# Low half of each split weight tile: negated high half from ScalarE plus an accumulating DMA, in place of a VectorE subtraction

## The chip, the core and the metric

The kernel runs on one core of one Trainium2 chip: TensorE (PE, matmuls, with its weight loads as PEld), VectorE (DVE), ScalarE (ACT), GpSimd (POOL) and SyncE (SP, which issues most DMAs), each with its own queue of instructions in a fixed order. The metric is the device time of one execution in microseconds; lower is better.

## The reference, cut to what matters

One decoder layer over 1024 tokens of width 1024 (`D_MODEL = SEQ = 1024`), in float32:

```python
h = rms_norm(x, g_norm)
proj = h @ w_in                       # RWKV, conv, attention inputs and merge gates: 97 tiles of 128 columns
y_rwkv = (o_rwkv * silu(rwkv_gate)) @ w_proj_rwkv      # after a scan over 16 heads of 64
y_conv = u @ w_proj_conv + b_proj_conv                 # after a causal depthwise conv of width 31
km, vm = split(rms_norm(mem, g_mem_norm) @ w_mem_kv)   # 256 memory tokens
y_mem = (att * silu(mem_gate)) @ w_proj_mem
y = gates[0] * y_rwkv + gates[1] * y_conv + gates[2] * y_mem
return x + y @ w_out                  # then a final rms_norm
```

## The kernel before, in words

All large matmuls are done to nearly float32 accuracy with operands rounded to fp32r: each operand is a sum of a high and a low half, and a product is three matmuls, high by high, high by low, low by high. For a weight tile `wf` (128 x 1024, 512 KB) the halves are `wh`, `wf` rounded to fp32r by an ACT copy, and `wl = wf - wh`.

A `Stream` (lines 131 to 163) brings weight tiles in a fixed order: `load` issues the DMA of `wf` on SP's queue, `split` makes `wh` and `wl`, `get` hands them to the matmuls, `ahead` prepares the next tile. There is one buffer for `wf` and two each for `wh` and `wl`, so the halves of tile n+1 go where those of tile n-1 were, and can be written only when the last matmul of tile n-1 is done. The main stream has 121 tiles; a second one (`kv_stream`, two `wf` buffers) has the 16 tiles of `w_mem_kv`.

`g_dense` (line 279) is one weight tile against 1024 tokens: two halves e of 24 matmuls of 512 columns (tile `d` in PSUM), called from generators that interleave it with other work. `g_kv` (line 867) uses a kv tile for only 24 matmuls of 256 columns (`g<-mH,wh`) or 12 of 512 (`ry<-wl,mH`). Instructions are handed over in the order in which the code runs, and a scheduler then sets the order on each engine.

The stages, by the profile's time: to about 49 us the norm of `x`; to about 1030 us the RWKV part, with its scan (`sav` L703, `sas` L710, `s` L713, group norm `vr` L114 and L118, `Y` L754, transposes L759) among dense tiles; then attention and the convolution, whose taps (`ac` L841) run on DVE and whose sum `csum` (L846, L848) on POOL, with the 16 kv tiles at 1059 to 1127 us; from about 1519 us the layer norm and the three branch projections with their loads; from about 1865 us the output projection.

Of the kernel before, what the change touches and what calls it, by code (L numbers as in the profile page):

```python
# [10 lines left out]
F32 = mybir.dt.float32  # L11
F32R = mybir.dt.float32r
AF = mybir.ActivationFunctionType
ALU = mybir.AluOpType
# [48 lines left out]
def hybrid_kernel(ctx: ExitStack, tc: tile.TileContext, x: bass.AP, mem: bass.AP, wt: bass.AP,  # L63
                  vecs: bass.AP, wup: bass.AP, gfin: bass.AP, out: bass.AP):
    nc = tc.nc
    act, dve, pool, pe = nc.scalar, nc.vector, nc.gpsimd, nc.tensor
# [7 lines left out]
    def bank(tag, bufs=1):  # L74
        return ps.tile([P, HS], F32, name=tag, tag=tag, bufs=bufs)
# [45 lines left out]
    def split_sb(src, hi, lo, scale=None, eng=None):  # L121
        if scale is None:
            act.copy(hi, src)  # L123
            (eng or dve).tensor_tensor(out=lo, in0=src, in1=hi.bitcast(F32), op=ALU.subtract)  # L124
        else:
            act.activation(hi, src, AF.Copy, scale=scale)
            dve.scalar_tensor_tensor(out=lo, in0=src, scalar=scale, in1=hi.bitcast(F32),
                                     op0=ALU.mult, op1=ALU.subtract)


    class Stream:
        def __init__(self, order, pl, raw=1, parts=2):
            self.order, self.n_dma, self.n_split, self.n_use = order, 0, 0, 0
            self.pl, self.bufs = pl, (raw, parts)
            self.raw, self.parts, self.eng = {}, {}, dve

        def load(self, upto):
            while self.n_dma < min(upto, len(self.order)):
# [5 lines left out]
        def split(self, upto):  # L144
            while self.n_split < min(upto, len(self.order)):
                self.load(self.n_split + 1)
                wh = self.pl.tile([P, D], F32R, name="wh", tag="wh", bufs=self.bufs[1])
                wl = self.pl.tile([P, D], F32R, name="wl", tag="wl", bufs=self.bufs[1])
                split_sb(self.raw.pop(self.n_split), wh, wl, eng=self.eng if self.n_split else dve)
                self.parts[self.n_split] = (wh, wl)  # L150
                self.n_split += 1

# [52 lines left out]
    stream = Stream(order, wp)  # L205
# [73 lines left out]
    def g_dense(idx, done, rh=None, rl=None, pre=None):  # L279
        wh, wl = stream.get(idx)  # L280
        rh, rl = (hH, hL) if rh is None else (rh, rl)
        for e in range(2):
            if pre is not None:
                pre(e)
            po = bank("d", 2)
            sl = slice(e * HS, (e + 1) * HS)
            n = 0
            for k in range(KT):
                ks_ = slice(k * P, (k + 1) * P)
                for l, r in ((wh, rh), (wh, rl), (wl, rh)):  # L290
                    pe.matmul(po, lhsT=l[:, ks_], rhs=r[:, k, sl], start=(n == 0), stop=(n == 3 * KT - 1))  # L291
                    n += 1
                    if n % 4 == 0 and n < 3 * KT:
                        yield
            if e == 0:
                stream.ahead()
            done(e, po)
            yield

# [20 lines left out]

    late = {}
    lo_gen = g_dense(T_LO, lambda e, po: late["lo"](e, po))
    with tc.tile_pool(name="prep", bufs=1, reuse_waits="tile") as pl:
        for i, _ in enumerate(g_norm(x, S, "g_norm", pl, hH, hL)):
# [4 lines left out]
    with tc.tile_pool(name="rk", bufs=1, reuse_waits="tile") as rk:  # L329
# [103 lines left out]
        def tile_job(kind, j):  # L433
            if kind == "lo":
                late["lo"] = done_lo
                return lo_gen
            if kind == "k":
                return g_dense(T_K + j, done_shift(KS, j, T_K, "ks", 2))
            if kind == "r":
                return g_dense(T_R + j, done_shift(RS, j, T_R, "rs", 3))  # L440
            if kind == "v":
                return g_dense(T_V + j, done_shift(VS, j, T_V, "v", 2))
            if kind == "g":
                return g_dense(T_RG + j, done_sg(j))
            return g_dense(T_M0 + j, done_m(j))
# [722 lines left out]
    with tc.tile_pool(name="wo1", bufs=1, reuse_waits="tile") as w1:  # L1168
# [12 lines left out]
        for fh in range(2):  # L1181
            fs = slice(fh * HS, (fh + 1) * HS)
            oh, ol = wo[fh]
            for t in range(KT):
# [10 lines left out]
                if fh == 1:  # L1195
                    rsqrt(rs[:, t:t + 1], ss[:, t, 1:2], 1.0 / D, e0[:, t:t + 1])
                    for h_ in range(2):
                        hs_ = slice(h_ * HS, (h_ + 1) * HS)
                        dve.scalar_tensor_tensor(out=xr[t][:, hs_], in0=xr[t][:, hs_], scalar=rs[:, t:t + 1],
                                                 in1=gf[:, hs_], op0=ALU.mult, op1=ALU.mult)  # L1200
# [46 lines left out]
```

## Time and profile before

| what | value |
|---|---|
| median of 3 runs (all) | 1961.22 us (1957.13, 1961.22, 1961.71) |
| the profiled execution, time and span | 1960.84 us, span 1959.0 us |
| mean granted TensorE clock | 0.991 |
| busy share of the span: PE, DVE, ACT, POOL | 94%, 72%, 35%, 12% |
| bytes read from HBM | 139.92 MB |
| `wh` copies on ACT, `wl` subtractions on DVE | 137 each |

A row of the profile names the line of the kernel, the engine, the operation, and what is written from what. A "busy" PE is one with a matmul in flight. Where a row of the timeline ends in [t <-X], the engine was idle for t us before it and X ended the wait.

### The profile page before, as it was taken

Reading aid. Unit: us, or ns where it says so; the run is one execution under the profiler, and the core shown is the slowest. Engines: PE = TensorE matmul, PEld = TensorE weight load, DVE = VectorE, ACT = ScalarE, POOL = GpSimd, SP = SyncE. Lnnn points to the kernel's source line nnn. Section 1 sums busy time; section 2 is a strip of 40 time slices with the busy share of each in tenths; the row PEclk is TensorE's granted clock in tenths of the full one; section 3 lists DMA queues with packets and bytes.
Section 4 is the critical chain, followed back from the end, with each engine's and each line's share of the span. In section 5 each row is a group of like instructions: output and inputs, shape, how many; then the busy total and the mean of one; then the engine's idle time right before and its main releaser. Section 6 shows DMA issues by size and latency. Waiting matters only on the chain. (4 is left out here: it accounts for less than half of the span.)

```text
span 1959.0 us, 30018 instructions
## 1 busy us (share of the span) xinstructions
PE 1848.2 (94%) x11412; PEld 1472.8 (75%) x11412; DVE 1411.1 (72%) x3028; ACT 693.2 (35%) x1303; POOL 226.5 (12%) x311
## 2 busy tenths in 40 slices
PE   6999998989899899989999999999999999999998
PEld 5777766767676676667788888888888787778887
DVE  6667787777778777787636998898999748644423
ACT  6334343443344344334334313232313435432121
POOL 2201111111111111111000000000000213100001
PEclk9999999999999999999999999999999999999999
DMA  4232212122121212212224411212123646775332
GB/s 147 58 97 63 71 36 68 54 61 68 48 86 36 66 56 58 71 42 79 71 78 140 132 46 42 75 54 76 54 76 108 233 163 221 256 252 164 129 129 86
DMA packets 127936, 188.61 MB, mean 96 GB/s; under 512 B 64432, under 2 KB 66608, under 8 KB 127792
## 3 DMA queue, kind: packets, MB, share of 16 engines
q1 hardware_dynamic: 122704, 178.11, 29.0%
q10 hardware_dynamic: 4768, 8.07, 1.1%
q8 instruction: 89, 1.46, 0.3%
q0 software_dynamic: 320, 0.52, 0.1%
q14 instruction: 55, 0.45, 0.1%
HBM read 139.92 MB, written 46.20 MB: 95 GB/s over the span
## 5 line engine op out<-in xcount | busy, mean ns | idle before, releaser
L291 PE MATMUL d<-hH,wh 128*128 128x512 f32 x1552 | 626.0, 403 | 6.8 <-DVE cg L928 4.4
L291 PE MATMUL d<-hH,wl 128*128 128x512 f32 x1552 | 621.8, 401 | 0.0
L291 PE MATMUL d<-hL,wh 128*128 128x512 f32 x1552 | 619.1, 399 | 0.0
L291 PEld LDWEIGHTS d<-hH,wh 128*128 128x128 f32 x1552 | 294.1, 189 | 63.6 <-DVE cg L928 5.7
L291 PEld LDWEIGHTS d<-hH,wl 128*128 128x128 f32 x1552 | 294.1, 190 | 59.4 <-issue 0.2
L291 PEld LDWEIGHTS d<-hL,wh 128*128 128x128 f32 x1552 | 294.1, 189 | 56.2 <-issue 0.2
L841 DVE SCALAR_TENSOR_TENSOR ac<-up,wdw,ac 128x1024 f32<-128x1024 f32 x240 | 308.2, 1284 | 11.8 <-ACT ac L838 6.0
L123 ACT CAST wh<-wf 128x1024 fp32r<-128x1024 f32 x137 | 143.6, 1049 | 324.1 <-PE d L291 304.3
L124 DVE TENSOR_TENSOR wl<-wf,wh 128x1024 fp32r<-128x1024 f32 x137 | 176.8, 1291 | 95.7 <-ACT wh L123 95.4
L291 PE MATMUL d<-oH,wh 128*128 128x512 f32 x384 | 152.5, 397 | 11.4 <-DVE mg L1101 7.4
L291 PE MATMUL d<-oH,wl 128*128 128x512 f32 x384 | 151.4, 394 | 0.0
L291 PE MATMUL d<-oL,wh 128*128 128x512 f32 x384 | 151.4, 394 | 0.0
L583 DVE TENSOR_TENSOR W<-W,tm 128x60 f32<-128x60 f32 (+24 forms) x496 | 112.4, 227 | 10.0
L580 DVE TENSOR_TENSOR tm<-W,U 128x60 f32<-128x60 f32 (+24 forms) x496 | 107.7, 217 | 11.1
L706 ACT ACTIVATE sp<-s,pc 128x128 f32<-128x128 f32 x120 | 48.3, 402 | 174.8 <-DVE s L713 137.6
L291 PEld LDWEIGHTS d<-oH,wh 128*128 128x128 f32 x384 | 72.9, 190 | 30.4 <-ACT y L1138 5.1
L710 PEld LDWEIGHTS sas<-sav,tk 128*128 128x128 f32 x240 | 38.4, 188 | 67.5 <-DVE sav L703 49.2
L710 PE MATMUL sas<-sav,tk 128*128 128x128 f32 x240 | 54.1, 307 | 34.1 <-DVE sav L703 32.4
L291 PEld LDWEIGHTS d<-oH,wl 128*128 128x128 f32 x384 | 72.8, 190 | 16.1
L291 PEld LDWEIGHTS d<-oL,wh 128*128 128x128 f32 x384 | 72.8, 189 | 15.4
L713 DVE SCALAR_TENSOR_TENSOR s<-sas,pc,sp 64x64 f32<-64x64 f32 x240 | 67.6, 282 | 21.5 <-PE sas L710 16.1
L703 DVE TENSOR_TENSOR sav<-ry,Y 64x128 f32<-64x128 f32 x128 | 36.8, 288 | 43.4 <-ACT Y L668 26.5
(277 smaller groups left out, 2608.7 us busy)
## 6 DMA issues: line engine op xcount, KB each, us to landing
wf<-in_wt_dram SPq DMA_DIRECT2D x137, 512.0 KB
g_d<-gt SPq DMA_DIRECT2D x48, 256.0 KB
U<-ud SPq DMA_DIRECT2D x64, 128.0 KB
nxt<-in_x_dram SPq DMA_DIRECT2D x8, 512.0 KB
o_rwkv_d<-o SPq DMA_DIRECT2D x16, 256.0 KB
cv_d<-ac SPq DMA_DIRECT2D x8, 512.0 KB
o_mem_d<-om SPq DMA_DIRECT2D x16, 256.0 KB
xs<-cv_d SPq DMA_DIRECT2D x8, 512.0 KB
```

The costliest lines, as they stand in the source:

```text
L123: act.copy(hi, src)
L124: (eng or dve).tensor_tensor(out=lo, in0=src, in1=hi.bitcast(F32), op=ALU.subtract)
L291: pe.matmul(po, lhsT=l[:, ks_], rhs=r[:, k, sl], start=(n == 0), stop=(n == 3 * KT - 1))
L580: dve.tensor_tensor(out=tv, in0=W[:, 0:m, i:i + 1].broadcast_to([NG * 32, m, n]), in1=U[:, i:i + 1, i + 1:32].broadcast_to([NG * 32, m, n] ...
L583: dve.tensor_tensor(out=wv_, in0=wv_, in1=tv, op=ALU.add)
L703: dve.tensor_tensor(out=sav[own, cc, :], in0=ry[own, cs], in1=Y[own, c // 2, :], op=ALU.add)
L706: act.activation(sp, S0, AF.Copy, scale=pc[:, c:c + 1])
L710: pe.matmul(sn[:, 0:P], lhsT=tk[:, cc, :], rhs=sav[:, cc, :], start=True, stop=True)
L713: dve.scalar_tensor_tensor(out=S1[vsl, vsl], in0=sn[vsl, vsl], scalar=pc[vsl, c:c + 1], in1=sp[vsl, vsl], op0=ALU.mult, op1=ALU.add)
L841: dve.scalar_tensor_tensor(out=ac, in0=up[:, tap:tap + S], scalar=wdw[:, tap * 8 + j:tap * 8 + j + 1], in1=ac, op0=ALU.mult, op1=ALU.add)
```

## The change

For every tile but the first of each stream, the subtraction on DVE is gone. ACT writes the low tile too, as `-wf` rounded to fp32r (which is `-wh`), and then a DMA issued from POOL adds the weights from HBM onto it. `wl` is therefore ready when that DMA has landed, and the weights are read from HBM twice. `stream.ahead()` is called after four matmuls of the first half of a tile instead of after all 24.

```diff
@@ class Stream, split @@
-                split_sb(self.raw.pop(self.n_split), wh, wl, eng=self.eng if self.n_split else dve)
+                wf = self.raw.pop(self.n_split)
+                act.copy(wh, wf)
+                if self.n_split:
+
+                    act.activation(wl, wf, AF.Copy, scale=-1.0)
+                    nc.gpsimd.dma_start(out=wl, in_=wt[self.order[self.n_split]], accum_op=ALU.add)
+                else:
+                    dve.tensor_tensor(out=wl, in0=wf, in1=wh.bitcast(F32), op=ALU.subtract)
@@ g_dense @@
                     n += 1
+                    if e == 0 and n == 4:
+                        stream.ahead()
                     if n % 4 == 0 and n < 3 * KT:
                         yield
-            if e == 0:
-                stream.ahead()
```

The lines below the first edit move down by 7 (L291 becomes L298, L212 becomes L219, L874 becomes L881, L114 to L124 stay).

On ACT, in the stage of the kv tiles, the program before had one cast for a kv tile (`wh_...` from `wf_...`) and the copy of a finished tile (`kmH`):

```order
L874 CAST kmH_10811<-g_11046 128x256
L874 CAST kmH_10811<-g_11081 128x256
L123 CAST wh_11141<-wf_11075 128x1024
L874 CAST kmH_10811<-g_11116 128x256
L123 CAST wh_11176<-wf_11110 128x1024
L874 CAST kmH_10811<-g_11151 128x256
```

Now, at the same place:

```order
L150 CAST wh_11203<-wf_11136 128x1024
L881 CAST kmH_10868<-g_11142 128x256
L153 ACTIVATE wl_11204<-wf_11136 128x1024
L150 CAST wh_11239<-wf_11172 128x1024
L881 CAST kmH_10868<-g_11178 128x256
L153 ACTIVATE wl_11240<-wf_11172 128x1024
```

The cast of a kv tile is followed by the copy of an earlier tile's result and only then by the negated copy, after which the DMA can be issued.

On PE, in the same stage, a kv tile's first matmuls (`wh`) stood a few dense matmuls ahead of its first one with `wl`, and one tile was finished before the next began:

```order
L212 MATMUL g_11116<-mH_10818,wl_11107 128x256
L212 MATMUL g_11151<-mH_10818,wh_11141 128x256
L212 MATMUL g_11151<-mL_10819,wh_11141 128x256
L291 MATMUL d_11415<-hH_174,wl_10974 128x512
L291 MATMUL d_11415<-hH_174,wh_10973 128x512
L291 MATMUL d_11415<-hL_175,wh_10973 128x512
L291 MATMUL d_11415<-hH_174,wl_10974 128x512
L291 MATMUL d_11415<-hH_174,wh_10973 128x512
L212 MATMUL g_11151<-mH_10818,wl_11142 128x256
```

Now the kv tiles go in pairs. The rows end at the first matmul with a `wl` of the pair; ahead of them stand two matmuls of its other tile (`wh_11131`) and ten dense ones:

```order
L298 MATMUL d_11488<-hH_174,wh_11012 128x512
L219 MATMUL g_11178<-mH_10875,wh_11167 128x256
L219 MATMUL g_11178<-mL_10876,wh_11167 128x256
L298 MATMUL d_11488<-hL_175,wh_11012 128x512
L298 MATMUL d_11488<-hH_174,wl_11013 128x512
L298 MATMUL d_11488<-hH_174,wh_11012 128x512
L298 MATMUL d_11488<-hL_175,wh_11012 128x512
L219 MATMUL g_11142<-mH_10875,wl_11132 128x256
```

The 22 matmuls left of the one tile and the 22 of the other follow without dense work between; the dense matmuls moved from between single tiles to between pairs (14, 12, 12, 12, 8 and 9 of them for the six pairs that have kv tiles behind them).

On POOL, in the RWKV stage, what stood about the two `vr` instructions of the group norm before:

```order
L567 MEMSET W_5529 128x256
L573 COPY W_5529<-rb_5530 32x8 x4
L114 TENSOR_SCALAR vr_5479<-vr_5479 128x8
L118 TENSOR_TENSOR vr_5479<-vr_5479,nhalf_97 128x8
L574 TENSOR_TENSOR U_5528<-U_5528,rb_5530 128x1024
```

and now:

```order
L574 MEMSET W_4331 128x256
L580 COPY W_4331<-rb_4332 32x8 x4
L154 DMA wl_4315<-in_wt_dram 128x1024
L114 TENSOR_SCALAR vr_4274<-vr_4274 128x8
L118 TENSOR_TENSOR vr_4274<-vr_4274,nhalf_97 128x8
L581 TENSOR_TENSOR U_4330<-U_4330,rb_4332 128x1024
```

The accumulating DMA of a tile stands ahead of the `vr` pair in POOL's queue, and waits there for its negated copy.

## Rows read from the trace of the kernel before

**Rows 1.** The page: busy time, share of the span, instructions
```profile
PE 1848.2 (94%) x11412; PEld 1472.8 (75%) x11412; DVE 1411.1 (72%) x3028; ACT 693.2 (35%) x1303; POOL 226.5 (12%) x311
```

**Rows 2.** Windows by stage: length, busy time of engines, PEclk, DMA share, GB/s
```profile
147.00:931.00 784.00, 719.97 (x5790) 546.14 (x5788) 607.63 (x1882) 309.12 (x658) 117.77 (x180) 0.99 0.22 60
1059.30:1127.00 67.70, 67.59 (x387) 59.08 (x386) 63.18 (x61) 27.58 (x36) 2.03 (x2) 1.00 0.39 125
1127.00:1519.00 392.00, 391.89 (x1848) 328.08 (x1847) 352.32 (x368) 113.14 (x212) 16.70 (x11) 1.00 0.20 67
1519.00:1764.00 245.00, 228.94 (x979) 183.18 (x978) 156.43 (x184) 97.67 (x127) 45.73 (x26) 0.98 0.68 225
1764.00:1865.00 101.00, 101.00 (x447) 83.46 (x446) 43.85 (x60) 19.65 (x26) 0.00 (x0) 1.00 0.43 141
```

**Rows 3.** Waits of PE, 147 to 931 us: total us, times, longest
```profile
PE sas L710 <- DVE sav L703: 30.7, 41, 1.8
PE tr L759 <- DVE Y L754: 19.1, 6, 3.3
```

**Rows 4.** Tiles wf and wl: count, duration ns (least/median/most), first and last start
```profile
L123 ACT CAST wh<-wf x137: 1030/1050/1059, 10.4 to 1842.9; 128x1024 fp32r<-128x1024 f32 x137
L124 DVE TENSOR_TENSOR wl<-wf,wh x137: 1210/1221/2854, 13.2 to 1844.4; 128x1024 fp32r<-128x1024 f32 x137
```

**Rows 5.** Timeline, one dense tile of the projections: start us, duration us
```profile
1766.58 1.05 ACT L123 CAST wh<-wf 128x1024 fp32r<-128x1024 f32 x1 [4.57 <-PE d L291]
...
1777.90 0.39 PE L291 MATMUL d<-oH,wl 128*128 128x512 f32 x1
```

**Rows 6.** Timeline, one kv tile
```profile
1074.40 0.37 ACT L874 CAST kmH<-g 128x256 fp32r<-128x256 f32 x1 [2.40 <-PE g L212]
1074.95 1.05 ACT L123 CAST wh<-wf 128x1024 fp32r<-128x1024 f32 x1 [0.18 <-DMA wf<-in_wt_dram]
1077.76 1.23 DVE L124 TENSOR_TENSOR wl<-wf,wh 128x1024 fp32r<-128x1024 f32 x1
1079.38 0.28 PE L212 MATMUL g<-mH,wl 128*128 128x256 f32 x1
1079.50 0.28 PE L212 MATMUL g<-mH,wh 128*128 128x256 f32 x1
```

**Rows 7.** DMA from POOL at 43.3 to 45.6 us; SP's load of wf, 71.4 on
```profile
43.38 0.51 POOL L404 DMA_DIRECT2D lox<-lot  x1 [0.93 <-DVE lot L402]
q0 software_dynamic: 128, 0.20, 43.8%
lox<-lot POOLq DMA_DIRECT2D x1, 128.0 KB, 2.2
1071.34 0.33 SPq L140 DMA_DIRECT2D wf<-in_wt_dram  x1
q1 hardware_dynamic: 144, 0.52, 48.5%
```

**Rows 8.** Timeline: csum on POOL, a late cast, and the tiles' first use
```profile
1353.26 2.40 POOL L848 TENSOR_TENSOR csum<-csum,ac 128x1024 f32<-128x1024 f32 x1 [53.65 <-DVE ac L841]
1360.58 0.39 PE L291 MATMUL d<-hH,wl 128*128 128x512 f32 x1
1723.81 1.04 ACT L123 CAST wh<-wf 128x1024 fp32r<-128x1024 f32 x1
1730.15 0.39 PE L291 MATMUL d<-oH,wl 128*128 128x512 f32 x1
```

**Rows 9.** Timeline, end of a scan; the last row is a window
```profile
296.76 1.23 DVE L124 TENSOR_TENSOR wl<-wf,wh 128x1024 fp32r<-128x1024 f32 x1
298.23 0.50 POOL L114 TENSOR_SCALAR vr<-vr 128x8 f32<-128x8 f32 x1 [12.10 <-DVE vr L748]
303.45 0.81 PE L759 MATMUL tr<-ident,Y 128*128 128x128 f32 x4 [3.25 <-DVE Y L754]
303.76:307.16 3.40, 3.40 (x14) 2.91 (x13) 1.50 (x2) 0.00 (x0) 0.00 (x0) 0.50 0.15 55
```

More of the change, by code (lines that the diff above doesn't have):

```diff
@@ L134, in __init__ @@
             self.pl, self.bufs = pl, (raw, parts)
-            self.raw, self.parts, self.eng = {}, {}, dve
+            self.raw, self.parts = {}, {}
         def load(self, upto):
```

## The prediction

> **What bounds the kernel now.** I read the page first: PE has a matmul in flight for 1848.2 of 1959 us, DVE is busy for 1411.1, ACT for 693.2, POOL for 226.5 [rows 1]. Shares over a whole kernel say little, so the windows by stage come next [rows 2]. PE has no gap at all in the stage of the kv tiles (67.59 of 67.70 us), in the stage behind it (391.89 of 392) and from 1764 to 1865 us (101.00 of 101). There DVE has free time, and work taken from it gives nothing. PE waits in two stages only: 64 us of the 784 us of the RWKV part, and 16 us of the 245 us of the projections. The waits of PE in the RWKV part name their causes [rows 3]: 41 waits, 30.7 us in all, for `sav`, and six, 19.1 us in all, for `Y`. Both are scan steps on DVE. So DVE's chain of small steps, not its sum of work, is what costs time, for some 50 us.
>
> The change gives DVE 135 subtractions of 1.22 us back, 165 us, and gives ACT 135 writes of the same shape as the cast, 1.05 us each, 142 us [rows 4]. ACT is busy for a third of the span and for 27.58 of 67.70 us in the kv stage [rows 1, 2], so 142 us more is room that it has. The question is what stands between the cast and the first matmul that needs `wl`: before, one subtraction; now a negated copy and then a DMA.
>
> **The price of the transfer.** I call X the time from POOL's issue to the landing. The trace has no accumulating DMA. The nearest row is a plain copy that POOL issues to a tile of halves: 128 KB land 2.2 us after the issue, and its 128 packets take 43.8% of 16 engines for 2.3 us, which is 1.0 us of all sixteen for 0.20 MB [rows 7]. By that rate 128 KB take 0.66 us and 512 KB 2.64 us, so X is 2.2 + 2.64 - 0.66 = 4.2 us. At the same moment SP reloads the `wf` that was just read: 0.52 MB for 48.5% of 3.6 us, 1.75 us of the sixteen engines [rows 7]. Shared in turn, that makes X = 5.9; I take **6 us**. If the DMA must read its target too, another 2.64 us go in: 8.6 us is the upper bound, 4.2 the lower. I take the middle one, since the sharing is in the order of the program and the second read is in no row.
>
> The Trainium skill, "Collectives: The Full Stack", section "The bandwidth ceiling: the fold count and why AG ≠ RS ≠ AR", states that an add in a DMA needs two source reads for each piece and moves half as fast as a copy. No run here shows it; by it X would be the upper bound, and the sum the upper end of my range.
>
> **Where X is hidden.** In the clean stage the slot of a tile came free 11.32 us before its first matmul with `wl` (cast at 1766.58, matmul at 1777.90) [rows 5]; a tile is 48 matmuls of 0.226 us (101 us, 447 of them [rows 2]), 10.85 us. After a cast and a negated copy of 1.05 us each [rows 4] there are 9.2 us for X. Six fits, and 8.6 fits too. So the main stream costs nothing where ACT and POOL are prompt. If X passed 9.2 us, each of some 27 such tiles would wait for the difference; that is a rival below. That `ahead` is called 20 matmuls earlier gains nothing there, as the cast already starts when the slot comes free.
>
> **Where it isn't: the kv tiles.** A kv tile is only 24 short matmuls, 0.12 us each (1079.38 to 1079.50) [rows 6]. The cast began at 1074.95, the subtraction ended at 1077.76 + 1.23 = 1078.99, the first matmul with `wl` ran at 1079.38: 0.4 us to spare [rows 6]. Now PE's order takes the kv tiles in pairs, and each tile's slot comes free when the tile two ahead is finished. So a pair's cycle is: cast 1.05, the copy `kmH` that now stands between (0.37), negated copy 1.05, X, and the 22 matmuls left of the tile (2.64), in all 5.11 + X = 11.1 us. PE's own work in a pair is 48 short matmuls (5.76) or 24 long ones (5.42) and the dense matmuls between the pairs, 14, 12, 12, 12, 8 and 9 of them at 0.226: 8.9, 8.5, 8.5, 8.1, 7.2 and 7.5, in all 48.7. Six pairs cost 66.7 - 48.7 = **+18 us**. At X = 4.2 it is 55.9 - 48.7 = +7, at 8.6 it is 82.3 - 48.7 = +34. Nothing behind PE hides it: this stage had 0.1 us of idle PE [rows 2], and what PE loses there it can't win back later.
>
> **The other terms.**
> RWKV, relief of DVE: 42 subtractions of 1.22 us are 51 of 784 us, 6.5% of the stage. If each DVE wait shrinks in that share, 6.5% of 50 us: **-3 us** (0 to -15, if the scan steps behind which a subtraction stood all move up). At the six ends of the scan it gives nothing: a subtraction at 296.76 stood ahead of the group norm's `vr` at 298.23 on POOL [rows 9]; now the accumulating DMA is queued ahead of `vr` on POOL and waits for a negated copy, 296.76 + 1.05 + 0.51 (the issue [rows 7]) = 298.32 at best. So PE's 3.25 us for `Y`, and the 3.4 us at half clock behind it [rows 9], stay.
> `csum` on POOL: at two of eight places it stands ahead of a tile's DMA, ended at 1353.26 + 2.40 = 1355.66, and the matmul came at 1360.58, 4.9 us later [rows 8]; at the other place 5.4. At X = 6: 1.1 + 0.6 = **+2 us** (0 to 7).
> The projections, 1519 to 1764 us: the DMA engines are already busy for 0.68 of the time there [rows 2], so I give X one us more, 7. Six tiles were cast late because their `wf` was late; the one shown has 1730.15 - (1723.81 + 1.04 + 1.05) = 4.2 us left [rows 8], the others, worked out alike, 5.6, 6.1, 6.9, 6.0 and 4.2. The lacks are 1.4 + 2.8 + 0.9 + 0.1 + 1.0 + 2.8 = **+9 us** (0 at 4.2; 25 at 9.6). The second read is 2.64 us of the engines for each tile of some 13 us, +0.2 on 0.68; other loads come later: **+4 us** (0 to 10).
> Clock: behind the 3.25 us gap PE ran 3.4 us at 0.50 [rows 9], which loses 1.7 us. New gaps of this length behind kv tiles and late tiles: two or so, **+3 us** (0 to 10).
>
> **Sum.** -3 + 18 + 2 + 9 + 4 + 3 = +33 us. The profiled execution took 1960.84 us, 0.4 under the median of 1961.22: 1960.84 + 33 = **1994 us**. The ends of the terms: -15 + 7 = -8, so 1953; and -3 + 34 + 7 + 25 + 10 + 10 = +83, so 2043.
>
> **The rivals.**
> *Hidden.* The transfer is bound by its fixed part. If POOL's 512 KB move at the rate of SP's load, 1.75 us [rows 7], X is 2.2 - 0.66 + 1.75 = 3.3 us. The kv cycle is then 8.4, six of them 50.5 - 48.7 = +2, the late tiles fit, DVE gives 3 back: 1960 us. For it: half of the small copy's 2.2 us is not movement. Against: the reload of `wf` and, perhaps, the second read.
> The Trainium skill, "DMA: Bandwidth & Descriptors", section "Anatomy of one DMA — SWDGE (gpsimd) path", gives about 2.0 us and bytes over 436 GB/s: 2.3 us for 128 KB, with which the 2.2 us of the trace agrees [rows 7], and 3.2 us for 512 KB, an estimate by that page; the sum would be 1960.
> *Faster.* The relief is worth more: PE's waits are for DVE, and a third of its 64 + 16 us of gaps closes (-25), with X no more than 4.2 (+7): 1943 us. It decides where the relief passes the kv stage's cost, at X = 4.2 from 7 us on. For it: all large waits name DVE [rows 3]. Against: a subtraction stands before few of those steps, and at the six longest the DMA on POOL takes its place [rows 9].
> *Every tile waits.* X passes 9.2 us, and the main stream is paced by the DMA. At X = 10: kv 90.7 - 48.7 = 42, 27 tiles by 0.8 = 22, `csum` and late tiles (X = 11) 10 + 33, clock 10, traffic 4, relief -3: +118, so about 2080 us. For it: nothing in the rows reaches 9.2. Against: nothing excludes it, as no row has such a DMA.
>
> **Chances.** Forecast 0.54, hidden 0.17, faster 0.13, every tile waits 0.16. A measurement here can tell 0.3%, about 5.9 us, from no change; so the forecast and the last rival are slower (0.70), hidden is the same (0.17), faster 0.13. The range leaves out the last rival alone and reaches from the faster case to the forecast's upper end: 1943 to 2043. The forecast's own is 1953 to 2043.
>
> **What would show it.** The landing of `wl` from the weights, by the table of DMA issues: 6 us after the issue in the kv stage, below 9 elsewhere. The kv stage longer than 67.7 us by some 18, with PE's waits there ended by that DMA. DVE's busy time down by some 165 us and ACT's up by some 142. In the RWKV part, PE's waits for `sav` and `Y` within a few us of before. In the projections the DMA share near 0.88, with waits for late `wl`. The prediction is wrong if X is under 4 or over 9 us, or if PE waits for the DMA in the clean stages.

## The result, and the profile after

The change made the kernel slower: 2086.17 us (median of 4, 2070.08 to 2091.77) against 1960.48 us for the kernel before in the same session (median of 4), a ratio of 1.063 with a 95% interval of 1.057 to 1.069. That is +126 us, where +33 was forecast and 2043 us was the upper end of the range. The profiled execution took 2087.05 us, its span 2085.4 us, with a mean granted TensorE clock of 0.970 where it had been 0.991.

From the page of the changed kernel: the busy line, which answers to [rows 1], the queues of SP (q1) and of POOL (q0) with packets, MB and share of 16 engines' span, and the issues of the new DMA with their median time to landing.

```profile
PE 1889.3 (91%) x11412; PEld 1496.5 (72%) x11412; DVE 1254.4 (60%) x2893; ACT 812.0 (39%) x1438; POOL 341.1 (16%) x446
q1 hardware_dynamic: 122704, 178.11, 27.9%
q0 software_dynamic: 19760, 71.31, 19.4%
wl<-in_wt_dram POOLq DMA_DIRECT2D x135, 512.0 KB, 7.7
```

DVE lost 157 us of work (165 forecast) and ACT gained 119 (142). PE's busy time rose by 41 us, from 1848.2 to 1889.3, with the same 11,412 matmuls: it ran more of them at half clock. A mean clock of 0.970 over 2085.4 us is a loss of 62.6 us, 0.991 over 1959.0 was 17.6: **45 us more lost to the half clock**. Idle PE is 1959.0 - 1848.2 = 110.8 us before and 196.1 after: **85 us more idle**. The 41 us of slower matmuls and the 85 us make up the 126; the rest of the 45 fell on a PE that was idle.

To see where, the two traces are cut at the same pieces of work: the starts of dense matmuls number 432, 2,406, 2,832, 2,930, 4,424, 5,365 and 5,807 (counted from 0) of the 5,808 that both kernels run. The kv stage so cut begins 6 us later than the window of [rows 2].

| stage | before, us | after, us | difference | forecast |
|---|---|---|---|---|
| up to the RWKV part | 148.8 | 152.6 | +4 | 0 |
| RWKV part | 782.3 | 823.9 | **+41.5** | -3 |
| up to the kv tiles | 134.4 | 144.6 | +10 | 0 |
| kv tiles | 61.7 | 100.0 | **+38.3** | +18 |
| behind them (taps, `csum`) | 391.9 | 394.9 | +3 | +2 |
| projections with loads | 245.0 | 268.3 | **+23.3** | +13 |
| last projection tiles | 100.3 | 106.4 | +6 | 0 |
| output projection | 94.6 | 94.6 | 0 | 0 |

Windows of the changed kernel over the RWKV part, the kv tiles, the stage behind them, the projections and the last tiles; columns as in [rows 2], which they answer to (length, then busy time of each engine, PEclk, DMA share, GB/s):

```profile
152.60:976.50 823.90, 733.63 (x5758) 554.57 (x5754) 554.72 (x1828) 341.10 (x700) 152.51 (x220) 0.96 0.37 83
1121.10:1221.10 100.00, 73.92 (x338) 61.16 (x337) 44.09 (x43) 37.39 (x47) 14.99 (x18) 0.88 0.72 164
1221.10:1616.00 394.90, 392.68 (x1847) 327.56 (x1846) 315.80 (x335) 140.40 (x241) 40.86 (x41) 1.00 0.45 106
1616.00:1884.40 268.40, 236.87 (x979) 186.30 (x978) 130.07 (x165) 116.68 (x148) 62.52 (x46) 0.96 0.82 241
1884.40:1990.80 106.40, 102.38 (x444) 83.93 (x443) 35.05 (x51) 26.72 (x34) 6.91 (x8) 0.98 0.67 184
```

PE is busy for 73.92 of 100.00 us in the kv stage, where it had no gap, and its clock there is 0.88. The clean stage behind stays clean: 392.68 of 394.90. In the RWKV part DVE has 53 us less to do than in [rows 2], and yet PE is idle for 90 us instead of 64, and its clock is lower.

The waits of PE over the whole span that name the new DMA (us in total, times, longest):

```profile
PE d L298 <- DMA wl<-in_wt_dram: 27.4, 14, 5.2
PE g L219 <- DMA wl<-in_wt_dram: 14.5, 3, 5.5
...
PE ry L894 <- DMA wl<-in_wt_dram: 11.5, 5, 3.8
```

They are 53 us in 22 waits, all of them behind the RWKV part. In the RWKV part PE's largest waits, to be held against [rows 3], are:

```profile
PE sas L717 <- DVE sav L710: 43.5, 39, 3.1
PE tr L766 <- DVE Y L761: 30.4, 12, 3.7
PE tr L615 <- DVE TT L607: 6.9, 9, 1.7
```

These grew without naming the DMA: the waits for `sav` (30.7 before) and `Y` (19.1), and a new one for `TT`.

The price X, from the list of the tile `wl` (ACT's negated copies with least/median/most duration in ns; then issue to landing in us):

```profile
L153 ACT ACTIVATE wl<-wf x135: 1044/1051/1106, 22.5 to 1970.2; 128x1024 fp32r<-128x1024 f32 x135
DMA to landing us min/median/max: 5.2/7.7/10.3
```

One cycle of a pair of kv tiles in the changed kernel's timeline, against [rows 6]:

```profile
1130.51 0.58 PE L219 MATMUL g<-mH,wl 128*128 128x256 f32 x1 [5.51 <-DMA wl<-in_wt_dram]
1130.89 0.42 PE L219 MATMUL g<-mH,wh 128*128 128x256 f32 x1
...
1135.44 1.05 ACT L150 CAST wh<-wf 128x1024 fp32r<-128x1024 f32 x1 [12.09 <-PE g L219]
1136.39 0.37 ACT L881 CAST kmH<-g 128x256 fp32r<-128x256 f32 x1
1136.65 1.07 ACT L153 ACTIVATE wl<-wf 128x1024 fp32r<-128x1024 f32 x1
1138.01 0.87 POOL L154 DMA_DIRECT2D wl<-in_wt_dram  x1 [13.51 <-ACT wl L153]
1146.11 0.56 PE L219 MATMUL g<-mH,wl 128*128 128x256 f32 x1 [4.46 <-DMA wl<-in_wt_dram]
```

The links are those of the forecast, in its order: cast, `kmH`, negated copy, issue, landing, matmuls. The cycle is 1146.11 - 1130.51 = 15.6 us instead of 11.1, for two reasons: X is 8.1 us here instead of 6, and the 22 matmuls that are left of the tile take 4.9 us (1130.51 to 1135.44) instead of 2.64. PE had waited 5.5 us for the landing, and then ran at half clock: the granted clock from 1130.5 to 1135.4 us is 0.50.

### The profile page after: what moved, and what is told of

The parts are those of the page before. It is cut to its first block, busy times and chain, and to the rows that moved or that the text cites. A ratio compares the mean times of both kernels' runs of the same rounds, so it can differ in the third digit from the quotient of the medians.

```text
span 2085.4 us, 30204 instructions
## 1 busy us (share of the span) xinstructions
PE 1889.3 (91%) x11412; PEld 1496.5 (72%) x11412; DVE 1254.4 (60%) x2893; ACT 812.0 (39%) x1438; POOL 341.1 (16%) x446
## 5 line engine op out<-in xcount | busy, mean ns | idle before, releaser
L298 PE MATMUL d<-hH,wh 128*128 128x512 f32 x1552 | 633.6, 408 | 9.7 <-DVE cg L935 5.7
L298 PE MATMUL d<-hH,wl 128*128 128x512 f32 x1552 | 632.3, 407 | 5.1 <-DMA wl<-in_wt_dram 5.1
L298 PE MATMUL d<-hL,wh 128*128 128x512 f32 x1552 | 624.9, 403 | 0.0
L298 PEld LDWEIGHTS d<-hH,wh 128*128 128x128 f32 x1552 | 298.2, 192 | 68.7 <-DVE cg L935 7.2
L298 PEld LDWEIGHTS d<-hH,wl 128*128 128x128 f32 x1552 | 297.9, 192 | 66.0 <-DMA wl<-in_wt_dram 6.8
L298 PEld LDWEIGHTS d<-hL,wh 128*128 128x128 f32 x1552 | 297.7, 192 | 57.0 <-issue 0.2
L154 POOL DMA_DIRECT2D wl<-in_wt_dram x135 | 119.0, 882 | 1161.0 <-ACT wl L153 812.3
L298 PE MATMUL d<-oH,wl 128*128 128x512 f32 x384 | 155.3, 404 | 22.4 <-DMA wl<-in_wt_dram 22.3
L298 PE MATMUL d<-oH,wh 128*128 128x512 f32 x384 | 154.3, 402 | 3.2 <-DVE mg L1108 1.8
L298 PE MATMUL d<-oL,wh 128*128 128x512 f32 x384 | 153.2, 399 | 0.0
L153 ACT ACTIVATE wl<-wf 128x1024 fp32r<-128x1024 f32 x135 | 142.4, 1055 | 21.9 <-PE ry L894 21.8
L298 PEld LDWEIGHTS d<-oH,wl 128*128 128x128 f32 x384 | 74.0, 193 | 43.4 <-DMA wl<-in_wt_dram 27.3
L717 PE MATMUL sas<-sav,tk 128*128 128x128 f32 x240 | 54.6, 310 | 46.7 <-DVE sav L710 44.3
L298 PEld LDWEIGHTS d<-oH,wh 128*128 128x128 f32 x384 | 74.2, 193 | 20.6 <-DVE g L1164 1.8
L720 DVE SCALAR_TENSOR_TENSOR s<-sas,pc,sp 64x64 f32<-64x64 f32 x240 | 67.6, 282 | 32.3 <-PE sas L717 25.7
L298 PEld LDWEIGHTS d<-oL,wh 128*128 128x128 f32 x384 | 74.2, 193 | 16.2
```

What stands on the lines that cost most here:

```text
L153: act.activation(wl, wf, AF.Copy, scale=-1.0)
L154: nc.gpsimd.dma_start(out=wl, in_=wt[self.order[self.n_split]], accum_op=ALU.add)
L717: pe.matmul(sn[:, 0:P], lhsT=tk[:, cc, :], rhs=sav[:, cc, :], start=True, stop=True)
L720: dve.scalar_tensor_tensor(out=S1[vsl, vsl], in0=sn[vsl, vsl], scalar=pc[vsl, c:c + 1], in1=sp[vsl, vsl], op0=ALU.mult, op1=ALU.add)
```

## The experiments

Theory A: the loss is the transfer, that is, waits for its landing and the half clock behind them. Its rivals: the new order that the earlier `ahead` gives the engines (B), ACT's extra copies (C), and what came up on the way. Each run stood beside the kernel before on the same chip; that had medians of 1960.3 to 1962.4 us.

| run | median, us (range) | ratio, 95% interval | RWKV stage (782.3 before) | kv stage (61.7 before) |
|---|---|---|---|---|
| the earlier call of `ahead` alone | 1984.5 (1982.9 to 1985.9) | 1.012 (1.010 to 1.013) | 800.3 | 61.7 |
| the accumulating DMA alone | 2127.9 (2113.8 to 2133.1) | 1.082 (1.078 to 1.087) | 865.3 | 102.0 |
| change, kv tiles by subtraction | 2044.9 (2039.1 to 2047.3) | 1.042 (1.040 to 1.044) | 816.9 | 61.9 |
| change without the DMA | 1980.1 (1975.1 to 1985.0) | 1.009 (1.006 to 1.012) | 791.7 | (see there) |
| change, plain copy for the DMA | 1984.2 (1982.6 to 1988.0) | 1.012 (1.011 to 1.014) | 782.7 | 70.2 |
| change, DMA on 16 partitions | 1991.5 (1987.6 to 2000.9) | 1.016 (1.013 to 1.019) | 805.3 | 67.6 |
| no DMA, `ahead` where it was | 1988.8 (1985.7 to 1992.8) | 1.015 (1.013 to 1.017) | 810.5 | (see there) |
| change, `U` on DVE | 2076.5 (2069.3 to 2082.3) | 1.058 (1.054 to 1.061) | 806.7 | 98.4 |
| before, `U` on DVE | **1953.6** (1953.6 to 1954.4) | 0.995 (0.993 to 0.997) | 775.6 | 61.7 |
| before, `Y` by `vr` on POOL | 1967.2 (1964.3 to 1972.4) | 1.002 (1.001 to 1.004) | 786.5 | 61.8 |
| change, DMA on half the columns | 2008.4 (1990.6 to 2012.8) | 1.021 (1.016 to 1.027) | 786.2 | 81.1 |

The two columns of stages come from the one profiled execution of each run, and executions of a run differ: the profiled one of the 16 partitions (2000.9 us) was the slowest of its four, that of half the columns (1990.6) the fastest.

**Each part alone.** The earlier call, on the kernel before:

```diff
+                    if e == 0 and n == 4:
+                        stream.ahead()
...
-            if e == 0:
-                stream.ahead()
```

> Only the earlier call of ahead, low halves still by the DVE subtraction, no second read. Theory A (the loss is the wait for the accumulating DMA and the half clock behind such waits): within 10 us of before, 1955 to 1970 us, the RWKV stage (784 us before, 825 after the change) within 5 us of 784. Theory B (the 41 us lost in the RWKV stage come from the other order that the earlier call gives the engines): RWKV stage 810 to 830 us, total 1990 to 2005 us, the kv stage still near 62 us.

It costs 24 us, more than theory A allowed and less than theory B expected, nearly all in the RWKV part (18) and ahead of the kv tiles (5). Waits of PE in its RWKV part:

```profile
PE tr L759 <- DVE Y L754: 34.5, 12, 3.9
```

Six waits for `Y` of some 3.2 us [rows 3] became twelve, six of 3.9 and six of 1.8. Nothing was added: the same instructions stand in another order. That PE now has fewer dense matmuls to run at the ends of the scan is likely, but not shown.

The DMA alone is the change with the old place of the call:

> The accumulating DMA, with ahead called where it was before. Theory A: as slow as the change or slower, 2080 to 2110 us, RWKV stage 820 us or more. Theory B: the RWKV stage back near 790 us, total about 2045 us. Both: the kv stage near 100 us, since it does not use the moved call.

At 2127.9 us it is slower than the change, by more than either theory had: 865.3 us for the RWKV part. So the two parts don't add up: the earlier call costs 24 us by itself, and saves 42 beside the DMA. Theory B as I put it (most of the RWKV loss is the call's) falls. Over its whole span PE waits 28.3 us for `TT` (10.4 in the change) and 51.0 for `sav` (44.3); which rows of the new order make it so slow isn't settled.

**The kv tiles apart.** A flag of the stream keeps the subtraction for the kv tiles:

```diff
-                if self.n_split:
+                if self.n_split and self.acc:
...
+    kv_stream = Stream([T_KM + i for i in range(16)], mp, 2, 2, acc=False)
```

> The change, but the 16 kv tiles get their low halves by the DVE subtraction again. Theory A and B alike: the kv stage returns from 100 to about 62 us, the PE waits for the DMA there vanish, and the rest stays: 2086 - 38 = 2048 us. If the kv loss came from elsewhere, it stays at 2080.

As expected to 3 us: the kv stage is back at 61.9 us. Its loss is local, the sum of it stands by itself.

**The transfer taken away.**

```diff
                     act.activation(wl, wf, AF.Copy, scale=-1.0)
-                    nc.gpsimd.dma_start(out=wl, in_=wt[self.order[self.n_split]], accum_op=ALU.add)
```

> The change without the accumulating DMA: the low half stays the negated high half, so the output is another one; ACT still writes both, DVE is still relieved, the second read is gone. Theory A: everything comes back, 1950 to 1965 us. Theory B: kv stage and projections come back (about 38 + 29 us), the RWKV stage stays at 820: about 2015 us. Theory C (the negated copies on ACT stand in the way of the scan's steps on ACT): the RWKV stage stays long here, but not in the run that only moves the call.

1980.1 us, between theory A (1950 to 1965) and theory B (2015): 106 of the 126 us go with the transfer, and 20 stay with what is left. In the RWKV part 9 of 41 us stay. (The kv stage can't be read alone here: the order moves dense matmuls from it to the stretch ahead of it, and both together take 203.6 us where they took 196.1.) So the transfer costs some 32 us in the RWKV part too, though no matmul there waited for its landing. The next two runs ask what of the transfer does it.

**The same order with other transfers.** A plain copy, or an accumulation onto 16 partitions alone, leave the rows of PE, ACT, DVE and SP exactly as in the change.

```diff
-                    nc.gpsimd.dma_start(out=wl, in_=wt[self.order[self.n_split]], accum_op=ALU.add)
+                    nc.gpsimd.dma_start(out=wl, in_=wt[self.order[self.n_split]])
```

> The change with the same DMA as a plain copy: the low half becomes the weights themselves, so the output is another one. The order of the instructions is that of the change on every engine. Theory A1 (the accumulation itself makes the transfer long, by a second access to the target): X, from issue to landing, falls from 7.7 us to about 4 to 5, total about 2020 us. Theory A2 (a 512 KB transfer of this queue takes that long whatever it does, beside the reload of wf): X stays at 7 to 8 us, total 2075 to 2090 us.

```diff
-                    nc.gpsimd.dma_start(out=wl, in_=wt[self.order[self.n_split]], accum_op=ALU.add)
+                    nc.gpsimd.dma_start(out=wl[0:16], in_=wt[self.order[self.n_split]][0:16], accum_op=ALU.add)
```

> The change with the DMA adding to 16 of the 128 partitions alone, an eighth of the bytes: the low half is wrong in the others, so the output is another one. The order on PE, ACT, DVE and SP is that of the change, and POOL differs in the shape alone. So what is left above before is order and ACT's part, what goes is the transfer's. Theory A (transfer): X about 2.5 us, kv stage 62 to 68 us, RWKV stage from 824 to about 792 as in the run without the DMA, round trip of the scan's small DMAs (W out and in again) from 6.2 back to about 4 us, total about 1985 us. Theory B (order): RWKV stage stays above 815 us, total about 2010 us.

The plain copy: POOL's queue, the issues, the landings, and the window of the RWKV part.

```profile
q0 software_dynamic: 19760, 71.31, 11.2%
wl<-in_wt_dram POOLq DMA_DIRECT2D x135, 512.0 KB, 4.9
DMA to landing us min/median/max: 3.8/4.9/8.4
153.30:936.00 782.70, 714.85 (x5758) 540.67 (x5754) 551.16 (x1828) 342.87 (x700) 140.39 (x220) 0.99 0.33 88
```

The accumulation onto 16 partitions, the same four:

```profile
q0 software_dynamic: 4640, 9.38, 2.9%
wl<-in_wt_dram POOLq DMA_DIRECT2D x135, 64.0 KB, 4.5
DMA to landing us min/median/max: 2.8/4.5/6.9
149.60:954.80 805.20, 730.22 (x5756) 553.17 (x5754) 555.63 (x1827) 342.57 (x700) 148.84 (x220) 0.96 0.24 62
```

With the same bytes from HBM, the same number of packets and the same order, the copy is 102 us faster than the accumulation. The packets of one 512 KB transfer keep the sixteen engines busy for 0.194 x 2085.4 / 135 = 3.00 us when they add, and for 0.112 x 1982.1 / 135 = 1.64 us when they copy: 1.83 times as long. Theory A1 is right that the adding makes the transfer long (total even below its 2020), A2 falls; what the engines do in the longer time no run shows. The Trainium skill, "Collectives: The Full Stack", section "The bandwidth ceiling: the fold count and why AG ≠ RS ≠ AR", gives for the adding step of a collective two source reads for each piece, and a factor of two; the 1.83 of this trace is near it.

But 64 KB, an eighth of the bytes, still take 4.5 us to land, and the RWKV part of that run is 22 us longer than the copy's, in the same order, with the lower DMA share (0.24 against 0.33). This doesn't fit theory A; theory B doesn't explain it either, since the order is the same. The 22 us are too many by some 10: the profiled executions of the two runs lie 17 us apart, their medians only 7. The difference shows at the end of a scan. The plain copy, then the 16 partitions:

```profile
827.24 0.69 DVE L761 TENSOR_TENSOR Y<-Y,vr 128x512 f32<-128x512 f32 x1 [2.16 <-POOL vr L118]
...
828.01 2.40 POOL L581 TENSOR_TENSOR U<-U,rb 128x1024 f32<-128x1024 f32 x1 [0.80 <-DMA U<-ud]
828.08 0.63 PE L766 MATMUL tr<-ident,Y 128*128 128x128 f32 x4 [1.48 <-DVE Y L761]
```

```profile
841.49 2.33 POOL L581 TENSOR_TENSOR U<-U,rb 128x1024 f32<-128x1024 f32 x1
841.54 2.83 DVE L761 TENSOR_TENSOR Y<-Y,vr 128x512 f32<-128x512 f32 x1 [2.15 <-POOL vr L118]
...
844.52 1.08 PE L766 MATMUL tr<-ident,Y 128*128 128x128 f32 x4 [3.61 <-DVE Y L761]
```

With the copy, `U` comes late enough that POOL begins to multiply it 0.77 us behind DVE's `Y`, which takes 0.69 us. Otherwise POOL begins 0.05 us ahead, and the same `Y` takes 2.83 us. PE then waits 3.61 instead of 1.48 us, and runs at half clock behind it (0.50 from 844.5 to 848.0 us). The same pair stands in the kernel before, at the end of the scan of [rows 9]:

```profile
300.41 2.34 POOL L574 TENSOR_TENSOR U<-U,rb 128x1024 f32<-128x1024 f32 x1
300.48 2.82 DVE L754 TENSOR_TENSOR Y<-Y,vr 128x512 f32<-128x512 f32 x1 [1.10 <-POOL vr L118]
```

`Y` is long 6 times of 16 in the kernel before, in the change and in the run with 16 partitions, 7 times where the call alone was moved, and never with the plain copy. In these traces what begins first decides: where the call alone was moved, `Y` once began 0.01 us ahead of `U` (782.35 us), and took 0.69 us while `U` took 2.93 instead of 2.34. The Trainium skill, "SBUF — State Buffer", section "Who interferes with whom", states that a DVE instruction with two inputs in SBUF contends with a GpSimd instruction that reads SBUF; both rows agree.

**The negated copy alone, in the old order of calls.** (change without the DMA, and without the earlier call)

> No accumulating DMA (another output) and ahead called where it was before: only the subtraction has gone from DVE and a negated copy come to ACT. If the relief of DVE is worth something by itself, as my rival said (-25 us), 1930 to 1950 us. If it is worth the -3 of my sum, 1955 to 1960. If each new order of the engines in the RWKV stage costs some 10 to 20 us, as the two runs before have it, 1965 to 1985 us.

1988.8 us, 28 us slower than before: the relief of DVE by itself is worth nothing that can be seen beside what comes with it, the copies on ACT and another order of the engines. (Its kv stage shares dense matmuls with the stretch ahead of it, as above.) Theory C, ACT's copies, isn't told apart from the order by this.

**The collision taken away.** The same line in both kernels (in these expectations theory C is the collision, D that it costs nothing):

```diff
-            pool.tensor_tensor(out=U, in0=U, in1=rb[:, None, :].broadcast_to([NG * 32, 32, 32]), op=ALU.mult)
+            dve.tensor_tensor(out=U, in0=U, in1=rb[:, None, :].broadcast_to([NG * 32, 32, 32]), op=ALU.mult)
```

> The change, with the multiplication of U by rb on DVE and no more on POOL, so that it can't run beside the group norm's last step Y (0.69 us alone, 2.83 us beside POOL's U, six of 16 times in the change). Theory C (this collision and the half clock behind it are a part of the 41 us of the RWKV stage): no Y above 1 us, RWKV stage 795 to 810 us, total 2060 to 2070 us. Theory D (the collision costs nothing, the longer transfers and the order do it all): RWKV stage 820 us or more, total 2080 to 2095 us.

> The kernel before with the same edit alone. Theory C: the six waits of 3.2 us for Y fall to about 1 us, most half-clock stretches behind them go: RWKV stage 760 to 770 us, total 1938 to 1950 us, faster than before. Theory D: within 6 us of before, or up to 20 us slower by another order of the engines.

Windows of the RWKV part, the change with this edit and the kernel before with it:

```profile
156.40:963.20 806.80, 728.21 (x5743) 550.64 (x5739) 553.58 (x1843) 342.53 (x699) 120.10 (x207) 0.97 0.38 85
```

```profile
148.50:924.10 775.60, 719.08 (x5742) 537.47 (x5738) 595.15 (x1895) 304.71 (x657) 87.25 (x166) 1.00 0.23 61
```

No `Y` is long in either. The RWKV part becomes 17 us shorter in the change, of which the later stages take back a part (2076.5, not the 2060 to 2070 expected), and 7 us in the kernel before, where the clock no longer falls. The edit also gives DVE more to do and changes the order of the engines, so the two numbers are not the collision's price alone. The second is the fastest version of this study: 1953.6 us, below both kernels, though not by as much as expected. A second way to part the two:

```diff
-            dve.tensor_tensor(out=yv, in0=yv, in1=vr[:, :, None].broadcast_to([P, n2, C]), op=ALU.mult)
+            pool.tensor_tensor(out=yv, in0=yv, in1=vr[:, :, None].broadcast_to([P, n2, C]), op=ALU.mult)
```

> The kernel before with the group norm's last multiplication (Y by vr) moved to POOL, behind the rsqrt that POOL does anyway and ahead of U, so that the two follow one another. The step becomes longer than 0.69 us (about 1.4 us, by the 128x256 operations of POOL at 0.75 us), but shorter than 2.82. Theory C: the long waits for Y shrink by about 1 us each, total 1945 to 1958 us. Theory D: 1960 us or more.

1967.2 us, a miss. The step took 1.04 us, but it takes that at every scan end; 14 waits, 1.8 us in the mean (25.4 in all), took the place of six of 3.2.

**Half the bytes.**

```diff
+                    nc.gpsimd.dma_start(out=wl[:, 0:HS], in_=wt[self.order[self.n_split]][:, 0:HS], accum_op=ALU.add)
```

> The change with the DMA adding to half of the columns alone, 256 KB, so that the output is another one; the order differs from the change in some 70 rows of PE's 7,765, in the kv stage. Theory A (what is lost beside the collision goes with the bytes of the accumulating transfer): X about 5.8 to 6.2 us, between the 4.5 of 64 KB and the 7.7 of 512 KB; RWKV stage between 805 and 824 us, kv stage about 80 us, projections about +10 us, total 2025 to 2040 us. If the loss has a threshold (a landing that must come before some point), the total lies near one of the ends, 1992 or 2086.

```profile
wl<-in_wt_dram POOLq DMA_DIRECT2D x135, 256.0 KB, 5.4
```

X is 4.5, 5.4 and 7.7 us at 64, 256 and 512 KB, and the kv stage 67.6, 81.1 and 100.0 us: it goes with X, as theory A says; the plain copy, 4.9 and 70.2 us, fits in. The total, 2008.4 us, is below the 2025 to 2040 that theory A expected. How the RWKV part goes with the bytes this run doesn't show: it is 786.2 us in the profiled execution (the shortest of the four, 1990.6 us; the others took 2004 to 2013), in which a single `Y` was long.

## Why the prediction was wrong

**Right.** What bounds the kernel, and that DVE's sum of work is not what costs time: 157 us less on DVE bought nothing that can be seen, with the DMA or without. The clean stage behind the kv tiles: 9.2 us of cover in a dense tile was enough for X (at most 8.0 us there), +3 us in 392. The kv stage as the place where PE can't hide the transfer, link by link.

**Right by luck.** No gain at the ends of the scan. I had `vr` wait on POOL behind the new DMA; in the change POOL had issued it and stood idle, and `vr` began 0.16 us behind the end of DVE's step (0.17 before):

```profile
370.57 0.20 POOL L114 TENSOR_SCALAR vr<-vr 128x8 f32<-128x8 f32 x1 [2.04 <-DVE vr L755]
```

What kept the waits for `Y` was the collision with `U`, which the prediction did not have, and they did not stay: 19.1 us became 30.4.

**The price of the transfer was mis-sized.** I took 6 us, between 4.2 for a plain copy and 8.6 if the target is read as well, "since the sharing is in the order of the program and the second read is in no row". The plain copy measured 4.9, the accumulation 7.7, and 8.1 in the cycle shown of the kv stage. The upper bound was near the truth; the second read, which I had set aside as not in a row, was the term that bore on it. In the kv term the measured 38 us are 26 of idle PE, where 18 were forecast, and 12 lost to the half clock, where this term had none: of the missing 20, 8 are the longer cycle and 12 the clock. X does not carry the miss by itself: with X at 8.6 and every other term at its end, my sum still stopped at 2043.

**The half clock was mis-sized.** I gave it 3 us (0 to 10) for two new gaps. It cost 45 us: each of the four waits of 3.8 to 5.5 us in the kv stage brought a stretch at half clock with it, which then lengthened the chain (4.9 us for 2.64) that led to the next wait, and in the RWKV part the windows' clock fell from 0.99 to 0.96. The forecast had two new gaps at 1.7 us; the clock falls to half 30 times in the changed kernel's trace, where it fell 10 times before.

**The RWKV term had the wrong sign, and that is the step that failed.** "6.5% of 50 us: -3 us" counted what DVE no longer does and nothing else. It came out at +41.5 us: 26 us more of idle PE, the rest slower matmuls. The runs show what stood in its place. First, the collision of `Y` with POOL's `U`: it was in the kernel before, as the six waits of 3.25 us [rows 3, 9], whose row shows a `Y` that the wait names and not why it is late; in the order of the change it costs some 17 us (the run with `U` on DVE), or 12 to 22 us (the 16 partitions against the plain copy, by medians and by the profiled executions). Some 7 of these the kernel before lost as well, so the collision is about 10 of the 41.5 us, an estimate. Second, the transfer: 32 of the 41.5 us go when the DMA is left out, and with no collision in either run the RWKV part is 806.7 us with the accumulation (`U` on DVE, so in another order) and 782.7 with the copy. No wait of PE there names the DMA, but the scan's own small transfers take longer. They go out to HBM and back (`wd` from `W`, then `wb` from `wd`, then `TT`). SP's waits for the first to land, in the RWKV part of the kernel before, the change, the plain copy and the 16 partitions:

```profile
SPq L596 <- DMA wd<-W: 7.0, 16, 0.7
```

```profile
SPq L603 <- DMA wd<-W: 18.6, 18, 2.7
```

```profile
SPq L603 <- DMA wd<-W: 7.4, 13, 1.6
```

```profile
SPq L603 <- DMA wd<-W: 1.9, 5, 0.9
```

From the issue of `wd` to that of `wb` the median is 3.8, 6.2, 4.8 and 4.0 us (56 times each), and 6.3 in the change with `U` on DVE. So the small transfers land later beside the larger ones. PE's waits for `TT`, the step behind them, go with it: 6.9 us in the change, 11.9 with `U` on DVE, and over the whole span 2.6 with the copy. That this delay makes up the whole of the rest isn't shown: no run delayed the small transfers alone, and what made the waits for `sav` grow by 13 us isn't told apart. Third, the order by itself: moving the call alone costs 18 us in this part, leaving out the DMA leaves 9, and leaving out the call as well 28. None of these orders was better than that of before.

**The projections** were right in kind: late tiles without cover, 14 waits for `wl`, all but one of them here and in the last tiles, and a DMA share of 0.82 (forecast 0.88). +23 and +6 us stand against 13; X was 8.1 us in the median where I had 7, and a part is again the half clock (0.96).

**The rivals.** *Every tile waits* came within 6 us of the time, at 2080, and for a wrong reason: in the clean stage behind the kv tiles X was at most 8.0 us, and its tiles waited once, for 0.9 us. *Hidden* supposed X = 3.3; even the plain copy needs 4.9, and it costs 24 us. *Faster* falls: without the DMA and without the earlier call the kernel is 28 us slower than before.

## What to carry to other kernels

Before giving an engine's work to a DMA, look for every chain that goes through a DMA, and not only for the tile that the new one makes: the scan's 32 KB round trips were hidden in no sum of mine. Price an accumulating DMA at nearly twice the engine time of a copy (1.83 here), and a long wait for it at half as much again (26 us of idle PE became 38 in the kv stage), since the clock fell behind the waits. Where a wait names an instruction, read that instruction's duration against its other executions: six executions of a step of 0.69 us took 2.82, and the run without them was 7 to 9 us faster than the kernel before, where the 135 subtractions taken from DVE bought nothing that can be seen.

## What the runs showed of the hardware that was not expected

An accumulating DMA had here, beside the reload of `wf`, a large part that doesn't go with the bytes: 64 KB land after 4.5 us (2.8 at the least), 512 KB after 7.7. How much of the 4.5 us is waiting for other transfers isn't told apart, and the 64 KB also go to fewer partitions. The Trainium skill, "DMA: Bandwidth & Descriptors", section "Anatomy of one DMA — SWDGE (gpsimd) path", gives 3.2 us for 512 KB, an estimate by its formula; the plain copy took 3.8 at the least and 4.9 in the median here, beside the reload of `wf`, and the measurement decides.

Whether DVE's `Y` takes 0.69 or 2.83 us hangs on less than a microsecond of another transfer's landing, and the RWKV part follows: with the plain copy, which reads 71 MB more from HBM and misses the collision, it is as short as in the kernel before (782.7 and 782.3 us).
